# Multi-query attention on one core: rounds of scores over tiles that come free on the way, a DMA that sums two terms, and more places for weights

## The chip, the cores and the metric

The kernel runs on one core of one Trainium2 chip. The metric is device time in microseconds (us) of one launch, the median of three runs. The profile is of one more execution of the same program, with a span from the first to the last instruction of the program and, around it, a little time of the device.

## The reference

Attention with 16 query heads that share one key and one value head:

```python
batch, seq_len, embed_dim = (8, 1024, 1024)
num_heads = 16                      # head_dim = 64
# q [8, 1024, 16, 64], k and v [8, 1024, 64], float32
q = q.transpose(0, 2, 1, 3)
scores = np.matmul(q, k[:, None].transpose(0, 1, 3, 2)) / np.sqrt(head_dim)
weights = np.exp(scores - np.max(scores, axis=-1, keepdims=True))
weights = weights / np.sum(weights, axis=-1, keepdims=True)
attn_out = np.matmul(weights, v[:, None])
return attn_out.transpose(0, 2, 1, 3).astype(np.float32)
```

## The kernel before

The work is cut into 1024 *units*. A unit u is one pair of heads (64 pairs over the 8 batches), one chunk of 512 queries (2 per pair) and one tile of 128 keys (8 per chunk): it yields a score tile of 128 keys x (2 heads x 512 queries) in PSUM. Eight units in a row with the same pair and chunk make one *head* h of the plan. There are three score tiles (sc0 to sc2, two banks each); the last two banks take the results.

**Scores** (`scores`, L263): two matmuls on TensorE (PE), one per head, each on 64 rows of the array. **Weights**: the exponential of a score tile is taken in one of two ways.

- A units: ScalarE (ACT) does the whole of it in one activation (`scalar_exp`, L276) to a `wt` tile in fp16, one of `N_WT` = 22 places.
- V units: VectorE (DVE) builds it from the bits of fp16. `ve_bits` (L283) reads the scores from PSUM and writes an integer whose bits, read as fp16, are a power of two times 1 + f. `ve_mantissa` (L294) takes out the mantissa m, `ve_power` (L304) the power of two, `ve_square` (L315) makes m squared, and the product of the first with m squared is split by columns: the first part on GpSimd (POOL; `ve_cube`, L319) while VectorE is in a pass that GpSimd can run beside, the rest on VectorE (`ve_rest`, L327). Three fp16 terms lie in one `w3` tile (8 places): bits, power, cube. The exponential is their sum with fixed factors.

**Values** (`value`, L396): for each of 8 groups (4 blocks of 128 queries x 2 heads) of a head, PE multiplies every term of the head's eight units by V, 65 columns with a column that sums the weights, and adds them up in PSUM. An A unit gives one term, a V unit three. The fixed factors of the terms are in copies of V: `vps` holds V times 1, C0 and C3, made by `prep_v` (L251) for each batch. Seven groups share a result bank. `inverse` (L345) takes the reciprocals of the sums, `finish` (L354) multiplies, both on VectorE, and a store (L380) goes out on SyncE's queue (SP). `last_values` (L420) does the last head.

Loads of q (L166, with a cast to fp16) and of v (L149) go through GpSimd's queue, the transposes of q (L176) and k through SP's. GpSimd's queue thus holds cubes and loads, in order.

**What sets the order.** `plan()` walks through the work with assumed durations (`T_PAIR`, `T_IN`, `T_OUT`, `T_MM`, `T_ACT`, `VE_COST` and so on), gives every instruction a due time, and sorts by it; each engine then runs its instructions in that order and waits on semaphores where data are not there. PE alternates between *rounds* of one or more score pairs and runs of values. A round begins where at least two score tiles are free at PE's time, or where one is free and ACT would otherwise run dry:

```python
n_free = sum(f <= t_pe for f in free)
go = n_free > 1
if n_free == 1:
    other = sorted(late_free(i) for i in range(3))[1]
    go = max(other, t_pe) + T_IN + T_SCORE > t_act + WAIT and t_pe + NEAR >= t_act - T_IN - T_SCORE
```

In a round of two the second unit can go to VectorE (`VSLOT` = 1), if VectorE's backlog and the quota (`RATE`) allow. Values of a term come up when its due time plus `SAFE` = 300 ns is past.

Of the kernel before, what the change touches and what calls it, by code (L numbers as in the profile page):

```python
# [10 lines left out]
FP32 = mybir.dt.float32  # L11
FP16 = mybir.dt.float16
I32 = mybir.dt.int32
I16 = mybir.dt.int16
ALU = mybir.AluOpType
# [3 lines left out]

SUM_LO = 128.0  # L20
SUM_HI = 60000.0
C0 = 0.9833984375
C3 = 0.163818359375
CS = 2.1471603163479376
N_WT = 22
N_W3 = 8
N_M = 2
N_M2 = 3
T_PAIR = 214.0
T_IN = 96.0  # L30
T_OUT = 106.0
T_MM = 29.6
T_SCORE = 480.0
T_ACT = 917.0
ACT_DONE = 1110.0
MM_DONE = 270.0
VE_TAIL = 115.0
# [3 lines left out]
GP_COL = 1.887  # L41
GP_TAIL = 230.0
T_LOAD = {"load_q": 640.0, "load_v": 1000.0}
SIDE = (("prep_k", 58), ("prep_v", 72))
VE_COST = {
    "bits": 1141.0,
# [8 lines left out]
    "finish": 542.0,  # L55
}
ORDER = {"bits": 0, "inverse": 1, "finish": 2}
NEXT = {"bits": 0.0, "inverse": 0.0, "finish": 0.0}
MINC = 128
REST = 768  # L60
LATE = 500.0
VSLOT = 1
DEFER = 12
HOLD = 1400.0
VE_SLACK = 2500.0
V_END = 12
RATE = 0.235
NEAR = 2000.0
WAIT = -100.0
T_BITS = 1255.0  # L70
SAFE = 300.0

# [2 lines left out]
def attention_main(ctx, tc, q, k, v, out, flag):  # L75
# [11 lines left out]
    nc = tc.nc  # L87
    B, S, H, D = q.shape
    P = 128
    NKT = S // P  # L90
    QCH = 512
# [25 lines left out]
    ident16 = consts.tile([P, P], FP16, name="ident16")  # L117
    ones = consts.tile([P, 1], FP32, name="ones")
    rec_all = consts.tile([P, NG], FP32, name="rec_all")
    vps = [consts.tile([P, 3, NKT, 72], FP16, name=f"vp{i}") for i in range(2)]  # L120
    ok_all = consts.tile([P, B + GRP], FP32, name="ok_all")
    qf = consts.tile([P, NKT, P], FP32, name="qf")

    sc = {}
    ve = {}
# [25 lines left out]
        )  # L151

    def load_q_first(p):
        q16[("first", p)] = consts.tile([P, NKT, P], FP16, name=f"q16_first{p}")
        src = q[0, :, 2 * p : 2 * p + 2, :].rearrange("(c p) h d -> p c (h d)", p=P)
        if p:
            nc.gpsimd.dma_start(out=q16[("first", p)], in_=src)
            return
        for cs in (slice(0, NKT // 2), slice(NKT // 2, NKT)):
            nc.scalar.dma_start(out=qf[:, cs, :], in_=src[:, cs, :])  # L160
# [86 lines left out]

    def prep_v(b):
        vp = kv[b]["vp"]
        for i, ci in ((1, C0), (2, C3)):  # L250
            x = nc.vector.tensor_scalar(  # L251
                out=vp[:, i, :, 0:D], in0=vp[:, 0, :, 0:D], scalar1=ci, scalar2=None, op0=ALU.mult
            )
        return x
# [23 lines left out]
    def ve_bits(u, i):  # L278
        p, c, j = where(u)
        w3 = w3p.tile([P, 3, 2, QCH], FP16, tag=f"w3_{i}", name=f"we{p}_{c}_{j}")  # L280
        wt[u] = [(w3[:, 1], 0), (w3[:, 0], 1), (w3[:, 2], 2)]
        ve[u] = {"w3": w3}
        nc.vector.tensor_scalar(  # L283
            out=w3[:, 1].bitcast(I16),
            in0=sc.pop(u),
            scalar1=15.0 * 1024,
            scalar2=0.0,
            op0=ALU.add,
            op1=ALU.max,
        )  # L290

    def ve_mantissa(u, i):
        ve[u]["m"] = mp.tile([P, 2, QCH], FP16, tag=f"m{i}", name=f"m{u}")
        return nc.vector.tensor_scalar(  # L294
            out=ve[u]["m"].bitcast(I16),
            in0=ve[u]["w3"][:, 1].bitcast(I16),
            scalar1=0x3FF,
            scalar2=0x3C00,
            op0=ALU.bitwise_and,
            op1=ALU.bitwise_or,  # L300
        )

    def ve_power(u):
        return nc.vector.tensor_scalar(  # L304
            out=ve[u]["w3"][:, 0].bitcast(I16),
            in0=ve[u]["w3"][:, 1].bitcast(I16),
            scalar1=0x7C00,
            scalar2=None,
            op0=ALU.bitwise_and,
        )  # L310

    def ve_square(u, i):
# [18 lines left out]
    def after_vector(x, key):  # L331
        tc.add_manual_dep(
            x.ins,
            made[key].ins.name,
            mybir.DependencyInfo(mybir.DependencyClass.Sync, mybir.DependencyReason.DATA),
            reason="GpSimd reads beside VectorE's next pass over PSUM",
        )

    def cube_of(u):
        w3 = ve[u]["w3"]  # L340
# [117 lines left out]
        return g0, min(GB, NG - GRP - g0)  # L458

    kinds = {}  # L460

    def terms_of(h):
        us = range(h * NKT, (h + 1) * NKT)
        own = [(u, 0) for u in us]
        return own + [(u, i) for i in (1, 2) for u in us if kinds[u] == "V"]

    def plan():
        ops = []

        def emit(t, what, *args):  # L470
            ops.append((t, len(ops), what, args))

        t_pe = t_ve = t_act = t_gp = 0.0
        mode = "v"
        u = 0
        free = [0.0] * 3
# [14 lines left out]
        behind = None  # L491
        t_behind = 0.0
        loads = []
        live = {}
        h = g = n = 0
        terms = None
# [11 lines left out]
        def slot():  # L508
            return min(range(3), key=lambda i: free[i])
# [7 lines left out]
        def backlog():  # L517

            t = sum(VE_COST[k] for k, _ in chain) + VE_COST["rest"] * len(left)
            return t + sum(VE_COST[k] for _, k, _, _ in evict)  # L520

        def share(s):

            nonlocal t_gp, lock, behind
            if behind is None:
                return
            v = next((v for v in left if left[v]), None)
            if v is not None:
                gs = max(t_gp, t_behind + GP_START, squared[v] + GP_START)
                n = min(int((s - gs - GP_FIX) / GP_COL) // 32 * 32, left[v])  # L530
                if n >= MINC:
                    lo = 2 * QCH - left[v]
                    emit(gs, "cube", v, lo, lo + n, behind)
                    left[v] -= n
                    lock = gs + GP_FIX + n * GP_COL
                    t_gp = lock + GP_TAIL
                    ready[v, 2] = max(ready.get((v, "g"), 0.0), t_gp)
                    ready[v, "g"] = ready.pop((v, 2))
                    for x in loads:
                        emit(t_gp, *x)  # L540
                        t_gp += T_LOAD[x[0]]
                    loads.clear()
            behind = None

        def vector_step(limit):

# [20 lines left out]
            if not urgent and (  # L567
# [22 lines left out]
                if what == "rest":  # L590
                    n = left.pop(v)
                    done = 0.0
                    if n:
                        emit(s, "rest", v, 2 * QCH - n)
                        t_ve = s + VE_FIX + n / 1.92
                        done = t_ve + VE_TAIL
                        behind, t_behind = ("rest", v), t_ve
                    ready[v, 2] = m2_used[live.pop(("m2", v))] = max(done, ready.get((v, "g"), 0.0))
                    return True
                chain.pop(0)  # L600
                t_ve = s + VE_COST[what]
# [44 lines left out]
                    chain.append(("check", b))  # L646
            return True

        def issue(t, first):
            nonlocal u, t_act, made_v  # L650
            i = slot()
            s = max(t, free[i])
            to_v = (
                first
                and NKT <= u < STEPS - V_END
                and not todo
                and max(t_ve, s) + backlog() < s + T_SCORE + VE_SLACK
                and kinds.get(u - 1) != "V"
                and made_v < (u - NKT + 1) * RATE
                and min(w3_used) < s  # L660
            )
            if not to_v and min(wt_used) == float("inf"):
                return False
            kinds[u] = "V" if to_v else "A"
            made_v += to_v
            emit(s, "score", u, i)
            done = s + T_SCORE
            free[i] = float("inf")
            if to_v:
# [26 lines left out]
        while h < H or u < STEPS:  # L696
            guard += 1
            assert guard < 400000

            while vector_step(t_pe):  # L700
                pass
            n_free = sum(f <= t_pe for f in free)
            go = n_free > 1
            if n_free == 1:
                other = sorted(late_free(i) for i in range(3))[1]
                go = max(other, t_pe) + T_IN + T_SCORE > t_act + WAIT and t_pe + NEAR >= t_act - T_IN - T_SCORE
            if u < STEPS and go:
                t = t_pe + (T_IN if mode == "v" else 0)
                k = 0
                while u < STEPS and k < n_free and issue(t, n_free > 1 and k == VSLOT):  # L710
                    t += T_PAIR
                    k += 1
                if k:
                    rounds += mode == "v"
                    mode = "s"
                    t_pe = t
                    continue
# [39 lines left out]
            idle += 20.0  # L757
        while vector_step(float("inf")):
            pass
        assert u == STEPS  # L760
        return [(what, args) for _, _, what, args in sorted(ops, key=lambda x: x[:2])]

# [18 lines left out]
    with tc.manual_schedule():  # L781
# [6 lines left out]
        for c in range(NKT):  # L788
            load_q(0, c)
        for t in vps:  # L790
            for i, ci in enumerate((1.0, C0, C3)):
                nc.gpsimd.memset(t[:, i, :, D : D + 1], ci)
        nc.vector.tensor_copy(out=ident16, in_=ident)
        nc.vector.memset(ones, 1.0)
# [13 lines left out]
        for c in range(NKT):  # L808
# [6 lines left out]
            "power": ve_power,  # L815
            "square": ve_square,
            "cube": ve_cube,
            "rest": ve_rest,
            "load_q": load_q,
            "load_v": load_v,  # L820
# [140 lines left out]
```

## Time and profile before

| | |
|---|---|
| time, median of 3 runs | 763.36 us (762.74 to 763.97) |
| profiled execution: time / span | 762.94 us / 761.1 us |
| granted TensorE clock, mean | 0.997 |
| A units / V units | 800 / 224 |
| score matmuls (L263), value matmuls (L396) | 2048, 11712 |
| GpSimd: cubes (L319), q loads (L166), v loads (L149) | 279, 64, 8 |
| first activation starts / last one ends | 7.0 us / 752.4 us |

The page gives for each engine its busy time, share of the span and instructions. Below that, a group's line has the source line, engine, operation, tile written and tiles read, shape, count, busy time in all, the mean length of one, and the engine's idle time before them with what ended it. Instructions of one engine overlap on PE, ACT and VectorE, so the length of one is more than the distance between two. A line of waits has who waited on whom, us in all, times, and the longest. A line of the timeline has its start, its length from the first start to the last end, and a count.

### The profile page before, as it was taken

What the parts mean: (1) busy time and instruction counts of PE and PEld (TensorE: products, weight loads), DVE (VectorE), ACT (ScalarE), POOL (GpSimd) and SP (SyncE); (2) the same over time, 40 slices, a digit from 0 to 9 for tenths busy, and PEclk for the clock granted to TensorE, in tenths of its full rate; (3) what the DMA queues carried; (4) which work ended last, traced back from release to release, by engine and by line L of the source; (5) the groups of instructions that cost most, each with busy time, mean ns of one, the idle gap of its engine ahead of it and who ended that gap; (6) DMA issues with size and microseconds to landing.
All of it is one profiled execution on the core that took longest, in us unless ns stands there. A gap on an engine that the chain in (4) does not pass through costs nothing.

```text
span 761.1 us, 31746 instructions
## 1 busy us (share of the span) xinstructions
PE 746.3 (98%) x13858; PEld 480.7 (63%) x13858; DVE 728.8 (96%) x1474; ACT 747.5 (98%) x803; POOL 327.2 (43%) x364
## 2 busy tenths in 40 slices
PE   6999999999999999999999999999999999999996
PEld 3566666666666666666666666666666665666665
DVE  4999999999999999999999999999999999999994
ACT  7999999999999999999999999999999999999995
POOL 4644444443444344543444344434444334444440
PEclk9999999999999999999999999999999999999999
DMA  9964437663466525665446563467535565211112
GB/s 173 167 121 99 99 64 114 113 117 94 78 118 113 105 62 112 106 113 92 79 93 112 114 113 74 90 111 125 99 75 95 100 112 96 71 44 58 30 58 73
DMA packets 168926, 73.91 MB, mean 97 GB/s; under 512 B 94032, under 2 KB 161616, under 8 KB 168784
## 3 DMA queue, kind: packets, MB, share of 16 engines
q1 hardware_dynamic: 149152, 53.76, 32.7%
q0 software_dynamic: 18576, 17.57, 18.3%
q8 instruction: 109, 1.79, 1.1%
q10 hardware_dynamic: 1056, 0.52, 0.2%
q14 instruction: 33, 0.27, 0.1%
HBM read 37.75 MB, written 33.55 MB: 94 GB/s over the span
## 4 chain that ended last, share of the span: by engine, by line
ACT 54%; PE 42%; issue 3%; DMA 1%; DVE 1%
ACT wt L276 54%; PE ot L396 24%; PE sc L263 17%; DMA knat<-in_k_dram 0%; PE otl L420 0%; DMA out_dram<-osb 0%; DVE osb L354 0%; PE kps L200 0%; PE qps L216 0%; DVE k L191 0%; DVE rec_all L345 0%; DVE k2t L212 0%; PE cnt L837 0%; DVE okm L835 0%; DVE ok_all L443 0%
## 5 line engine op out<-in xcount | busy, mean ns | idle before, releaser
L276 ACT ACTIVATE wt<-sc 128x1024 f16<-128x1024 f32 x800 | 745.0, 1046 | 1.1 <-PE sc L263 0.9
L319 POOL TENSOR_TENSOR we<-we,mm 128x448 f16<-128x448 f16 (+4 forms) x279 | 281.9, 1010 | 409.2 <-DVE mm L315 214.4
L396 PE MATMUL ot<-vp,wt 128*128 128x65 f16 x6336 | 432.2, 194 | 0.0
L396 PE MATMUL ot<-vp,we 128*128 128x65 f16 x5376 | 432.2, 194 | 0.0
L396 PEld LDWEIGHTS <-wt 128*128 128x128 f16 x6336 | 317.4, 97 | 115.0 <-issue 115.0
L396 PEld LDWEIGHTS <-we 128*128 128x128 f16 x5376 | 316.1, 97 | 104.5 <-issue 103.4
L263 PE MATMUL sc<-qt,k2t 64*128 64x512 f16 x2048 | 354.3, 385 | 4.4 <-ACT wt L276 2.9
L283 DVE TENSOR_SCALAR we<-sc 128x1024 int16<-128x1024 f32 x224 | 272.5, 1217 | 8.7 <-PE sc L263 6.7
L315 DVE TENSOR_TENSOR mm<-m 128x1024 f16<-128x1024 f16 x224 | 151.8, 678 | 0.0
L263 PEld LDWEIGHTS <-k2t 64*128 64x128 f16 x2048 | 80.1, 93 | 48.5 <-issue 7.8
L294 DVE TENSOR_SCALAR m<-we 128x1024 int16<-128x1024 int16 x224 | 92.5, 413 | 0.2
L304 DVE TENSOR_SCALAR we<-we 128x1024 int16<-128x1024 int16 x224 | 92.5, 413 | 0.0
L354 DVE TENSOR_TENSOR osb<-ot,rec_all 128x448 f32<-128x448 f32 x146 | 89.2, 611 | 0.2
L327 DVE TENSOR_TENSOR we<-we,mm 128x576 f16<-128x576 f16 (+7 forms) x222 | 87.4, 394 | 0.0
L166 POOL DMA_DIRECT2D q<-in_q_dram x64 | 38.6, 606 | 5.5 <-issue 1.5
L345 DVE RECIPROCAL rec_all<-ot 128x7 f32<-128x7 f32 x146 | 28.7, 197 | 7.4 <-PE ot L396 6.8
L149 POOL DMA_DIRECT2D vp<-in_v_dram x8 | 7.2, 899 | 0.0
L251 DVE TENSOR_SCALAR vp<-vp 128x512 f16<-128x512 f16 x16 | 3.8, 279 | 2.2 <-DMA vp<-in_v_dram 2.2
L200 PE MATMUL kps<-ident,k 128*64 128x128 f16 x16 | 1.3, 314 | 4.4 <-DVE k L191 4.3
L234 DVE TENSOR_SCALAR k16d<-knat 128x1024 f16<-128x1024 f32 x7 | 4.7, 672 | 0.0
L229 DVE COPY qt<-qps 128x512 f16<-128x512 f16 (+1 forms) x2 | 1.1, 555 | 3.0 <-PE qps L216 3.0
L200 PEld LDWEIGHTS <-k 128*64 128x64 f16 x16 | 0.8, 158 | 4.6 <-DVE k L191 4.6
(30 smaller groups left out, 23.7 us busy)
## 6 DMA issues: line engine op xcount, KB each, us to landing
out_dram<-osb SPq DMA_DIRECT2D x109, 256.0 KB, 2.6
q<-in_q_dram POOLq DMA_DIRECT2D x56, 256.0 KB, 4.4
out_dram<-osb SPq DMA_DIRECT2D x38, 128.0 KB, 2.4
knat<-in_k_dram SPq DMA_DIRECT2D x7, 256.0 KB, 3.9
q<-in_q_dram POOLq DMA_DIRECT2D x8, 192.0 KB, 8.2
vp<-in_v_dram POOLq DMA_DIRECT2D x8, 128.0 KB, 5.8
qt<-q SPq DMA_TRANSPOSE x64, 4.8
qf<-in_q_dram ACTq DMA_DIRECT2D x2, 256.0 KB, 4.0
```

The source lines that it names most:

```text
L166: nc.gpsimd.dma_start(out=q16[(b, c)], in_=q[b, c * P : (c + 1) * P, h0:, :].rearrange("p h d -> p (h d)"),)
L263: nc.tensor.matmul(sc[u][:, hh, :], k2t[r : r + 64, j * P : (j + 1) * P], qt[b][r : r + 64, p % HP, c * QCH : (c + 1) * QCH], start=True, ...
L276: nc.scalar.activation(out=w, in_=sc.pop(u), func=EXP, scale=escale, bias=math.log(CS))
L283: nc.vector.tensor_scalar(out=w3[:, 1].bitcast(I16), in0=sc.pop(u), scalar1=15.0 * 1024, scalar2=0.0, op0=ALU.add, op1=ALU.max,)
L294: return nc.vector.tensor_scalar(out=ve[u]["m"].bitcast(I16), in0=ve[u]["w3"][:, 1].bitcast(I16), scalar1=0x3FF, scalar2=0x3C00, op0=ALU.b ...
L304: return nc.vector.tensor_scalar(out=ve[u]["w3"][:, 0].bitcast(I16), in0=ve[u]["w3"][:, 1].bitcast(I16), scalar1=0x7C00, scalar2=None, op0 ...
L315: return nc.vector.tensor_tensor(out=ve[u]["m2"], in0=m, in1=m, op=ALU.mult)
L319: x = nc.gpsimd.tensor_tensor(out=wu[:, lo:hi], in0=we[:, lo:hi], in1=mm[:, lo:hi], op=ALU.mult)
L327: return nc.vector.tensor_tensor(out=wu[:, lo:], in0=we[:, lo:], in1=mm[:, lo:], op=ALU.mult)
L345: nc.vector.reciprocal(out=rec_all[:, g0 : g0 + n], in_=o[:, 0:n, D])
L354: nc.vector.tensor_tensor(out=ob[:, i0 : i0 + n, :], in0=o[:, 0:n, 0:D], in1=rec.unsqueeze(2).broadcast_to([P, n, D]), op=ALU.mult,)
L396: nc.tensor.matmul(ots[g0][:, gg - g0, 0 : D + 1], w[:, hh, qb * P : (qb + 1) * P], kv[h // (HP * NCH)]["vp"][:, ci, u % NKT, 0 : D + 1], ...
```

## The change

It has these parts, all in the attention's main function and its plan:

- **Terms of V units.** The mantissa is set between 0.5 and 1 (0x3800 for 0x3C00), the power term gets fixed low bits by a second operation (`| 0x0201`), and the factors become: bits times KAPPA, power times 1, cube times 1. V is held in two copies (1, KAPPA) and not three; `prep_v` makes one scaled copy per batch.
- **A sum by DMA.** Of every three V units one is put in `merged`: after its cube is made, a DMA of GpSimd's queue adds its power term to its cube term (`merge`), and its values then have two terms and not three. The plan counts 650 ns of GpSimd for it and takes the sum as there 5000 ns after its issue.
- **Rounds.** A tile counts as free if it will be so, by the plan, within 90 ns of PE's time for the first, and for each next one within 50 ns of the time its pair comes up in the round. The unit for VectorE is the second of a round of two or more. A single V unit may also be a round by itself if ACT has over 1200 ns in stock and VectorE is ahead.
- **Places.** 27 for ACT's weights. The first q tiles lie in places of the wt and w3 rings that are not yet used, not in tiles of their own.
- **Constants** of the plan: durations, backlog (`VE_SLACK`), quota (`RATE` 0.24), when a rest pass is due (`REST` 576), and others.

In the order that comes out there are 802 A and 222 V units, 74 of these merged, 11088 value matmuls, and 641 rounds of scores for 744. The core of the diff:

```diff
-C0 = 0.9833984375
-C3 = 0.163818359375
-CS = 2.1471603163479376
-N_WT = 22
+KAPPA = 1.5258396029178207
+CS = 3.2766468288976904
+N_WT = 27
...
-T_PAIR = 214.0
+T_PAIR = 215.5
-T_OUT = 106.0
-T_MM = 29.6
+T_OUT = 120.0
+T_MM = 30.2
-T_ACT = 917.0
+T_ACT = 905.0
+T_MERGE = 650.0
+MERGED = 5000.0
+ADD_N = 1
+ADD_M = 3
...
-REST = 768
-LATE = 500.0
-VSLOT = 1
+REST = 576
+LATE = 0.0
+EPS = -1000000000.0
+AWAY = 1200.0
+SLACK1 = -500.0
+SOON = 50.0
+FIRST = 90.0
-HOLD = 1400.0
-VE_SLACK = 2500.0
+HOLD = 1000.0
+VE_SLACK = 1800.0
-RATE = 0.235
-NEAR = 2000.0
-WAIT = -100.0
+RATE = 0.24
+NEAR = 400.0
+WAIT = 200.0
...
-        for i, ci in ((1, C0), (2, C3)):
+        for i, ci in ((1, KAPPA),):
...
-        wt[u] = [(w3[:, 1], 0), (w3[:, 0], 1), (w3[:, 2], 2)]
+        wt[u] = [(w3[:, 1], 1), (w3[:, 0], 0), (w3[:, 2], 0)]
...
-            scalar2=0x3C00,
+            scalar2=0x3800,
...
             scalar1=0x7C00,
-            scalar2=None,
+            scalar2=0x0201,
             op0=ALU.bitwise_and,
+            op1=ALU.bitwise_or,
...
+    def merge(u):
+        w3 = ve[u]["w3"]
+        nc.gpsimd.dma_start(out=w3[:, 2], in_=w3[:, 0], accum_op=ALU.add)
...
         own = [(u, 0) for u in us]
-        return own + [(u, i) for i in (1, 2) for u in us if kinds[u] == "V"]
+        own += [(u, 1) for u in us if kinds[u] == "V" and u not in merged]
+        return own + [(u, 2) for u in us if kinds[u] == "V"]
...
+        def merge():
+            nonlocal t_gp
+            done, v = merges.pop(0)
+            s = max(t_gp, done)
+            emit(s, "merge", v)
+            t_gp = s + T_MERGE
+            ready[v, 2] = s + MERGED
...
-            n_free = sum(f <= t_pe for f in free)
+            t_in = t_pe + (T_IN if mode == "v" else 0.0)
+            n_free = 0
+            for f in sorted(free):
+                if f > (t_in + n_free * T_PAIR + SOON if n_free else t_pe + FIRST):
+                    break
+                n_free += 1
             go = n_free > 1
+            slack = VE_SLACK if go else None
             if n_free == 1:
                 other = sorted(late_free(i) for i in range(3))[1]
                 go = max(other, t_pe) + T_IN + T_SCORE > t_act + WAIT and t_pe + NEAR >= t_act - T_IN - T_SCORE
+                if t_act > t_in + AWAY and wants(t_in, SLACK1):
+                    go = True
+                    slack = SLACK1
             if u < STEPS and go:
-                t = t_pe + (T_IN if mode == "v" else 0)
+                t = t_in
                 k = 0
-                while u < STEPS and k < n_free and issue(t, n_free > 1 and k == VSLOT):
-                    t += T_PAIR
+                at_v = int(n_free > 1 and t + T_PAIR + T_SCORE > t_act + EPS)
+                while u < STEPS and k < n_free and issue(t, slack if k == at_v else None):
+                    t = t_now + T_PAIR
                     k += 1
```

## The prediction

> **What bounds the kernel now.** I read the busy times of the page first, then the busy times by stretch, the waits, and last the ACT and PE timelines. Busy shares alone do not tell:
>
> ```profile
> PE 746.3 (98%) x13858; PEld 480.7 (63%) x13858; DVE 728.8 (96%) x1474; ACT 747.5 (98%) x803; POOL 327.2 (43%) x364
> ...
> L276 ACT ACTIVATE wt<-sc 128x1024 f16<-128x1024 f32 x800 | 745.0, 1046 | 1.1 <-PE sc L263 0.9
> ```
>
> PE and ACT both look full. The stretches (PE, PEld, DVE, ACT, POOL, clock, DMA share, GB/s) say that it is so all the way:
>
> ```profile
> 60.00:160.00 100.00, 99.91 (x1871) 64.37 (x1869) 98.72 (x203) 99.99 (x109) 42.88 (x44) 1.00 0.53 100
> 460.00:560.00 100.00, 99.84 (x1871) 64.38 (x1869) 98.27 (x200) 100.00 (x109) 44.13 (x51) 1.00 0.52 95
> ```
>
> But ACT's activations overlap: one lasts 1046 ns and there is one per 745.4 us / 800 = 931 ns, so a late start hides inside the one before. ACT's timeline shows two paces:
>
> ```profile
> 7.00 7.44 ACT L276 ACTIVATE wt<-sc 128x1024 f16<-128x1024 f32 x8 [0.70 <-PE sc L263]
> ...
> 399.65 6.69 ACT L276 ACTIVATE wt<-sc 128x1024 f16<-128x1024 f32 x7
> ```
>
> At the start, with scores in stock, eight take 7.44 us: (7.44 - 1.1)/7 = 0.905 us each. In the middle seven take 6.69: (6.69 - 1.05)/6 = 0.940. Start to start no two are closer than 903 ns. The 217 activations whose scores ended within 800 ns of the start of the one before follow it at 907 ns on average; for the other 582 of 799 they ended later. So ACT is being fed late, by 24 ns apiece, and the feeder is PE. PE waits for nobody:
>
> ```profile
> PE sc L263 <- ACT wt L276: 2.9, 8, 0.5
> ...
> PE sc L263 <- DVE we L283: 0.8, 3, 0.3
> ```
>
> 3.7 us in all. Joining each score with the last reader of its tile, the tile has been free for 434 ns (median) when PE comes to it. **PE's order is the bound; tiles, ACT and VectorE are not.** What PE spends is in its timeline:
>
> ```profile
> 319.70 0.23 PE L396 MATMUL ot<-vp,wt 128*128 128x65 f16 x2
> 319.86 0.39 PE L263 MATMUL sc<-qt,k2t 64*128 64x512 f16 x2
> 320.18 0.20 PE L396 MATMUL ot<-vp,wt 128*128 128x65 f16 x1
> 320.22 0.32 PE L396 MATMUL ot<-vp,we 128*128 128x65 f16 x5
> 320.37 0.26 PE L396 MATMUL ot<-vp,wt 128*128 128x65 f16 x3
> ```
>
> Five values take 320.37 - 320.22 = 0.15 us, 30 ns each (31.2 over all 10968 steps). A round of one score pair: about 125 ns from the last value's start, 3 ns between the two matmuls, 316 to the next value, 443 in all. A further pair in the same round adds 226. So a round's turn-round costs 443 - 226 - 31 = 186 ns, once, however many pairs it holds.
>
> **The change, part by part.** Counts come from the two kernels' instruction orders.
>
> PE, values. 74 of the 222 V units have power and cube summed by a DMA, so one term fewer each: 74 x 8 = 592 matmuls; two V units fewer (222 for 224, each with two terms beyond its own) take 2 x 2 x 8 = 32 more. 11712 becomes 11088; 624 x 31.2 ns = 19.5 us off.
>
> PE, rounds. Before: 475 rounds of one pair, 264 of two, 5 longer: 744. After: 293 of one, 336 of two, 12 longer: 641. 103 x 186 ns = 19.2 us off. PE's own work is then 746.3 - 19.5 - 19.2 = 707.6 us, all of it on the path that sets the end until ACT takes over. A round now starts up to 90 ns before its first tile is due and up to 50 before the next: at most 641 x 90 ns of waiting, but PE waits there because ACT or VectorE is behind, which is spare time of PE and not of the path.
>
> ACT: 802 activations for 800. At 907 ns, 727.4 us; at today's 931.5, 747.1. PE at 708 no longer sets the pace, so **what is late next is ACT itself**. I take 912 ns: one activation in five still late by today's 24 ns, since about a fifth of the score pairs go to VectorE and shift the tiles' turn. 802 x 0.912 = 731.4 us.
>
> VectorE: two V units less, 2 x (1217 + 413 + 413 + 678) = 5.4 us; the rest passes (L327) have 99360 columns for 107488, at (684 - 305)/(1024 - 288) = 0.515 ns a column 4.2 us, and three passes fewer 0.5; eight prep_v passes fewer (one copy of V scaled, not two) 8 x 279 = 2.2. 728.8 - 12.3 = 716.5, of which about 5 lie before the first and after the last activation: 711 of 731, 97%. Least intervals between starts, summed, give some 706. It has room, but little.
>
> GpSimd: 247 cubes of 127968 columns for 279 of 121888. By the 448 (1029) and 736 (1578) rows: 1.906 ns a column, 175 fixed, so +11.6 - 5.6 = 6 us. 74 merges have no row; the nearest is the q load L166, 592 ns mostly, up to 742 beside a whole L304 pass: 74 x 0.6 = 44 us. Sum 377, half the span. Behind a waiting merge stand cubes and q loads, and PE's cube terms wait for those; the merge stands in the order after its rest pass is due, and 50% idle covers a late one. At 742 each it costs 11 us more there, nothing on the path.
>
> The merge's landing is the price that no row shows. It is 256 KB in 128 rows through GpSimd's queue, and PE's first value of that term waits for it with every later value and score queued behind. Bounds:
>
> ```profile
> q<-in_q_dram POOLq DMA_DIRECT2D x56, 256.0 KB, 4.4
> ...
> vp<-in_v_dram POOLq DMA_DIRECT2D x8, 128.0 KB, 5.8
> ...
> k2t<-k16d SPq DMA_TRANSPOSE x7, 2.7
> ```
>
> 2.7 us below (SBUF to SBUF), 6.7 above (the slowest V load after 50 us). The q load is nearest: same queue, same 2048-byte packets (172 ns, 8 on each engine), and it too reads 4096 bytes for each 2048 written, as an addition of two fp16 rows does. I take 4.4 us (5th to 95th of a hundred: 3.7 to 5.6). By the plan's due times the first use comes 5.3 to 11.0 us after issue, median 6.7. With landing x for all, the stalls of PE add up to 0 at 5.0, 1.5 us at 5.5, 10 at 5.9, 18 at 6.2, 34 at 6.7; ACT's stock bridges about 0.2 us of each. So nothing at 4.4. In the first 40 us, where the DMA engines are full, one q load took 8.1 us: a merge there may cost 2.8, which goes in the range.
>
> The Trainium skill, Collectives: The Full Stack, section The bandwidth ceiling, says an addition in a DMA emits two read descriptors per chunk on one ring and so takes twice as long as a copy. By it, as an estimate, a merge would have 16 packet times on an engine and not 8, 1.4 us more.
>
> Two copies of V, q's first tiles in places of the wt and w3 rings (read before 10 us, overwritten after 20), 27 places for 22, the second operation in the power pass (L294 has two and takes the same 413 ns as L304 with one): nothing. Longer keeping of weights only makes PE's choice of values wider.
>
> **Sum**, against the profiled execution (span 761.1, 762.94 with 1.84 around it; 0.4 under the median 763.36): first activation at 7.0, 731.4, 0.1 for the last one's length, then 761.1 - 752.4 = 8.7 of last values and stores: 747.2; with 1.84, 749.0.
>
> **Rivals.** (a) ACT is fed perfectly, 905 ns: 743.4, and 741.8 at 903. For it: eight in a row at the start did. Against: three tiles, of which VectorE holds one much of the time. Part of the forecast's spread, as is 920 ns (755.5), the next cluster of intervals in the trace.
> (b) Merges land 1.4 us later than q loads, at 5.8: stalls of 8 us, 757. For: a packet with two reads may take two packet times. Against: SBUF answers both, not HBM. That is the page's rule worked out; no run here has shown a merge.
> (c) Slower: merges land late enough to take the whole gain. 764.5 needs 15.5 us of stalls, which is a landing of 6.1 us; at 6.7 it is 749 + 34 - 5 = 778. Place: PE at the first cube value of a merged unit, then ACT. For: the slowest V load did 6.7, two reads and a write in one packet are unseen. Against: 51 q loads stayed under 5.9, and the DMA engines are half idle, 74 x 8 x 172 ns = 102 us adding 14% to 53%.
> (d) The gain does not come: with three tiles, one at VectorE, a tile's loop (written, waited for, read, freed) sets ACT's pace, and it stays at 931: 7.0 + 747.1 + 8.8 + 1.84 = 764.7, same or just slower. Against: tiles wait 434 ns for PE today, not the other way round.
> (e) The rounds do not shrink: excluded, the order has them.
>
> **How the numbers follow.** Forecast with (a): 0.74; (b) 0.10; (c) 0.11; (d) 0.05. Forecast 749. Range 742 (903 ns) to 761 (920 ns and (b)'s stalls, or 912 and a few late merges): it leaves out (c), most of (d). A difference of 0.2%, 1.5 us, is about what the runs can tell (762.74 to 763.97). Faster: forecast and (b), 0.84; same: half of (d), 0.03; slower: (c) and the rest of (d), 0.13.
>
> **What would show it.** Right: ACT's interval at 905 to 918 in the stretches (109 or 110 per 100 us instead of 107.4 starts), PE waiting on ACT's tiles for 10 to 25 us where it waits 3.7 now, no PE wait on a we DMA over 0.3 us. Wrong: merges landing after 5.8 us with PE weight loads waiting on DMA (b, c); PE waits on tiles large and ACT still at 930 (d); VectorE's bits passes starting late with VectorE at 99% would mean that VectorE, not ACT, has become the bound.

## The result and the profile after

The changed kernel takes 783.59 us (median of 4 runs, 779.38 to 785.07); the kernel before, on the same chip, 763.66 us (762.74 to 764.01). The ratio is 1.0254 [1.0209, 1.0299]: slower, where 749.0 and faster was forecast. The profiled execution took 782.14 us, with a span of 780.4 and a mean granted clock of 0.976 (0.997 before).

The page of the changed kernel, busy times and the groups of ACT and of the merge (line, engine, operation, tiles, count | busy us, mean ns | idle before, with what ended it):

```profile
PE 730.8 (94%) x13234; PEld 474.2 (61%) x13234; DVE 734.0 (94%) x1455; ACT 743.9 (95%) x805; POOL 402.5 (52%) x404
...
L289 ACT ACTIVATE wt<-sc 128x1024 f16<-128x1024 f32 x802 | 741.4, 1147 | 18.4 <-PE sc L276 17.5
...
L355 POOL DMA_DIRECT2D we<-we x74 | 67.6, 913 | 74.2 <-issue 20.5
```

PE was 98% busy and is 94%; no engine is full any more. ACT, which had been idle for 1.1 us before its activations, is idle for 18.4. The stretches (PE, PEld, DVE, ACT, POOL, clock, DMA share, GB/s) show that the loss is not spread evenly:

```profile
60.00:160.00 100.00, 93.96 (x1715) 60.85 (x1715) 98.87 (x194) 97.45 (x106) 51.94 (x51) 0.98 0.71 125
...
460.00:560.00 100.00, 93.12 (x1670) 60.68 (x1671) 91.72 (x185) 93.31 (x103) 52.93 (x52) 0.97 0.67 121
```

A count in this view takes in activations that only reach into the stretch. By their starts there are 105 and 102 in 100 us, where 109 or 110 were forecast; and the clock, 1.00 before, is 0.98 and 0.97. The stretches between (160 to 360) hold 109 starts each at 1.00. So there are places where it goes wrong. The waits (waiter <- whom it waited for: us in all, times, longest):

```profile
ACT wt L289 <- PE sc L276: 17.5, 28, 5.3
...
PE sc L276 <- ACT wt L289: 11.9, 28, 0.5
PE sc L276 <- DVE we L296: 11.8, 23, 1.4
...
PE ot L414 <- DMA we<-we: 10.1, 6, 5.0
```

PE waits for ACT's tiles as forecast (10 to 25 us). One wait is new: 10.1 us for the merges' landing, six times and up to 5.0 at a time. Another has grown: 11.8 us for tiles that VectorE still holds, where it was 0.8.

**Where 33.1 us went** (782.14 against 749.0). First activation's start to the last one's end is 759.1 us for a forecast 731.5: 27.6. After it come 75 values, where the forecast's tail, taken from before, held 4 (2.2 us more), and a longer drain of GpSimd at the program's end (3.3). The first of these was taken apart by experiments.

### The profile page after: what moved, and what is told of

Same layout as the page of the kernel before. It is cut to its first block, busy times and chain, and to the rows that moved or that the text cites. A ratio compares the mean times of both kernels' runs of the same rounds, so it can differ in the third digit from the quotient of the medians.

```text
span 780.4 us, 30889 instructions
## 1 busy us (share of the span) xinstructions
PE 730.8 (94%) x13234; PEld 474.2 (61%) x13234; DVE 734.0 (94%) x1455; ACT 743.9 (95%) x805; POOL 402.5 (52%) x404
## 4 chain that ended last, share of the span: by engine, by line
PE 45%; DVE 38%; DMA 7%; issue 6%; ACT 3%; POOL 0%; DVEq 0%; POOLq 0%; SPq 0%
PE ot L414 26%; PE sc L276 19%; DVE we L296 14%; DVE mm L329 7%; DMA we<-we 5%; DVE m L307 5%; DVE we L341 4%; DVE we L317 4%; DVE osb L372 3%; ACT wt L289 3%; DVE rec_all L363 1%; DMA out_dram<-osb 1%; DMA qf<-in_q_dram 0%; PE otl L438 0%; DVE k16d L247 0%
## 5 line engine op out<-in xcount | busy, mean ns | idle before, releaser
L289 ACT ACTIVATE wt<-sc 128x1024 f16<-128x1024 f32 x802 | 741.4, 1147 | 18.4 <-PE sc L276 17.5
L333 POOL TENSOR_TENSOR we<-we,mm 128x448 f16<-128x448 f16 (+10 forms) x247 | 297.4, 1206 | 279.3 <-DVE mm L329 84.0
L414 PE MATMUL ot<-vp,wt 128*128 128x65 f16 x6352 | 416.3, 195 | 0.0
L414 PE MATMUL ot<-vp,we 128*128 128x65 f16 x4736 | 401.6, 195 | 10.3 <-DMA we<-we 10.1
L276 PE MATMUL sc<-qt,k2t 64*128 64x512 f16 x2048 | 353.9, 389 | 25.5 <-ACT wt L289 11.9
L414 PEld LDWEIGHTS <-we 128*128 128x128 f16 x4736 | 294.5, 98 | 92.8 <-issue 89.2
L296 DVE TENSOR_SCALAR we<-sc 128x1024 int16<-128x1024 f32 x222 | 269.0, 1212 | 12.8 <-PE sc L276 11.5
L276 PEld LDWEIGHTS <-k2t 64*128 64x128 f16 x2048 | 93.0, 93 | 93.2 <-issue 50.7
L355 POOL DMA_DIRECT2D we<-we x74 | 67.6, 913 | 74.2 <-issue 20.5
L307 DVE TENSOR_SCALAR m<-we 128x1024 int16<-128x1024 int16 x222 | 100.1, 451 | 0.2
L317 DVE TENSOR_SCALAR we<-we 128x1024 int16<-128x1024 int16 x222 | 98.2, 442 | 0.0
L341 DVE TENSOR_TENSOR we<-we,mm 128x576 f16<-128x576 f16 (+16 forms) x219 | 87.2, 398 | 0.0
```

The source lines that it names most:

```text
L276: nc.tensor.matmul(sc[u][:, hh, :], k2t[r : r + 64, j * P : (j + 1) * P], qt[b][r : r + 64, p % HP, c * QCH : (c + 1) * QCH], start=True, ...
L289: nc.scalar.activation(out=w, in_=sc.pop(u), func=EXP, scale=escale, bias=math.log(CS))
L296: nc.vector.tensor_scalar(out=w3[:, 1].bitcast(I16), in0=sc.pop(u), scalar1=15.0 * 1024, scalar2=0.0, op0=ALU.add, op1=ALU.max,)
L307: return nc.vector.tensor_scalar(out=ve[u]["m"].bitcast(I16), in0=ve[u]["w3"][:, 1].bitcast(I16), scalar1=0x3FF, scalar2=0x3800, op0=ALU.b ...
L317: return nc.vector.tensor_scalar(out=ve[u]["w3"][:, 0].bitcast(I16), in0=ve[u]["w3"][:, 1].bitcast(I16), scalar1=0x7C00, scalar2=0x0201, o ...
L333: x = nc.gpsimd.tensor_tensor(out=wu[:, lo:hi], in0=we[:, lo:hi], in1=mm[:, lo:hi], op=ALU.mult)
```

## The experiments

Three causes were tested. **G**, GpSimd's queue: a merge holds GpSimd for longer than planned, and the cube behind it then runs beside VectorE passes that it blocks. **L**, the landing: PE stands at the first value of a merged unit. **C**, the clock: what G and L make PE wait lowers its granted clock, which costs again. Beside them stand that the rounds (**R**), places or constants of the plan are to blame, and that the order itself costs (**W**), because PE runs out of values while the plan counts a sum as under way. "After" below is the changed kernel; each diff is against it.

### The same order without the DMAs, and the plan without merges

The first of these leaves the power term out of the merged units' sums.

```diff
 x4_same_order_no_dma
     def merge(u):
         w3 = ve[u]["w3"]
-        nc.gpsimd.dma_start(out=w3[:, 2], in_=w3[:, 0], accum_op=ALU.add)
+        return
 e2_no_merges
-ADD_N = 1
+ADD_N = 0
```

> The changed kernel's own order, instruction for instruction, with the 74 additions by DMA left out (so the power term is missing from the merged units' sums). PE, ACT, VectorE and the cubes stand as planned, with the plan's 5000 ns of waiting still in the order. If the loss is the DMAs themselves, by GpSimd's time (G) and late landings (L): 746-753, the forecast's own price of the rest. If the order costs, because PE is made to run out of values while a sum is counted as under way (W): 757-766, with PE waiting on tiles for 20 us or more and low-clock stretches in the middle.

> The changed kernel with no V unit merged (ADD_N = 0): three terms each with two copies of V, 11680 value matmuls, new rounds and places kept. G and L: no blocked passes (under 1 us as before), no PE wait on a we DMA, clock low only at the start and the end; PE's own work 708 + 592 x 31.2 ns = 726 us, ACT the bound: 750-758. R: the loss stays, 770-785.

The same order of instructions without the 74 DMAs took 757.87 us (757.65 to 758.7), ratio 0.9929 [0.9912, 0.9945]. **The DMAs alone cost 783.59 - 757.87 = 25.7 us.** The time lies above the 746 to 753 expected if the DMAs were the whole loss, at the lower end of W's range; of W's signs, PE waits 15.9 us for tiles by the view of waits (20 or more expected), and one stretch has the low clock. The page of x4_same_order_no_dma, and one of its stretches:

```profile
PE 729.0 (96%) x13234; PEld 475.1 (63%) x13234; DVE 719.2 (95%) x1455; ACT 738.5 (98%) x805; POOL 332.4 (44%) x330
```

```profile
60.00:160.00 100.00, 97.69 (x1786) 63.53 (x1782) 98.13 (x199) 100.00 (x111) 45.13 (x44) 1.00 0.57 101
```

ACT is full, 111 where after has 106. VectorE is busy for 719.2 us where after has 734.0 for the same passes: 14.8 us of VectorE's time are made by the merges. But even this is 9 us above the forecast of 749.0, mostly by ACT's run of 738.9 us, 921 ns apiece and not 912.

With no merges in the plan either (665 rounds, 11680 values): 759.2 us (758.89 to 759.49), ratio 0.994 [0.9924, 0.9957], 1.2 us over what was expected if G and L are the loss, and far from R's 770 to 785.

### The merge in GpSimd's queue, with nobody waiting for it

Here the DMA adds into a spare tile that no one reads; the V units keep three terms. In the first it reads the power term, which has long been there; in the second the cube term, so that it must wait for the rest pass, as the real one does. The order is the same in both. The third is the second with 1400 ns planned for the merge.

```diff
 e6_merge_unused, e9_merge_of_cube_unused, x3_merge_of_cube_unused_priced
+    spare = consts.tile([P, 2, QCH], FP16, name="spare")
...
-        nc.gpsimd.dma_start(out=w3[:, 2], in_=w3[:, 0], accum_op=ALU.add)
+        nc.gpsimd.dma_start(out=spare, in_=w3[:, 0], accum_op=ALU.add)   # e6
+        nc.gpsimd.dma_start(out=spare, in_=w3[:, 2], accum_op=ALU.add)   # e9, x3
...
-T_MERGE = 650.0
+T_MERGE = 1400.0   # x3 alone
-N_WT = 27
+N_WT = 26
```

> The DMA's additions are issued as in the changed kernel, 74 of them with the same 650 ns in the plan, but into a spare tile that nothing reads; V units keep three terms (11680 value matmuls), so PE waits for no merge; 26 places for weights, not 27, to make room. G: blocked passes as in the changed kernel, 14-20 us, VectorE busy 732-737, time 765-772. L: 750-758, as without merges. R: 778-785.

> As the run whose additions go to a spare tile, but the DMA reads the cube term and not the power term: so, as in the changed kernel, a merge waits at the head of GpSimd's queue for its rest pass. T_MERGE = 650; V units keep three terms, PE waits for no merge; 26 places. G: blocked passes 14-20 us (3.1 when the merge read the power term), which is then the price of the wait in GpSimd's queue alone: time 767-774 against 763.3. L: blocked passes or not, 762-765, since ACT and PE ride over late score tiles as long as PE itself never stands.

> The run whose additions read the cube term into a spare tile (771.9 us), with T_MERGE = 1400: G alone, priced in full. Blocked passes from 23.6 us to under 4, and 760-764, as when the DMA read the power term (763.3); the rest over 757-759 is the longer drain of GpSimd at the end. If a merge in GpSimd's queue costs even where the plan knows of it: 766-771.

Measured: 763.3 us (ratio 0.9993 [0.9983, 1.0003]), 771.9 (1.0112 [1.0091, 1.0132]) and 761.52 (0.9975 [0.9964, 0.9985]). The merge's group of e6_merge_unused, and then of e9_merge_of_cube_unused with its busy times:

```profile
L356 POOL DMA_DIRECT2D spare<-we x74 | 68.9, 931 | 2.3 <-PE sc L277 1.7
```

```profile
PE 740.6 (96%) x13826; PEld 490.3 (64%) x13826; DVE 739.2 (96%) x1453; ACT 742.6 (96%) x805; POOL 399.2 (52%) x418
...
L356 POOL DMA_DIRECT2D spare<-we x74 | 67.7, 915 | 69.5 <-issue 21.4
```

The issue itself is the same, 0.92 us. (That the first is 4 us slower than e2_no_merges is for the most part a longer drain of GpSimd at the program's end, 4.7 us for 1.5. It hit none of its three ranges: G's expected 14 to 20 us of blocked passes and got 3.1, because this merge finds its term ready; the second run was made to tell the issue from the wait.) What differs is the wait at the head of the queue, 2.3 us in all against 69.5, and it costs 771.9 - 763.3 = **8.6 us though no one waits for the data**. With the merge planned at 1400 ns the 8.6 us are gone, though in a plan of its own (73 merges, 650 rounds for 663), and VectorE's busy time falls back from 739.2:

```profile
PE 741.1 (98%) x13778; PEld 490.0 (64%) x13778; DVE 719.1 (95%) x1441; ACT 741.2 (98%) x808; POOL 373.3 (49%) x387
```

This third run also moves as many bytes by DMA as the changed kernel (93 MB, 74 in e2_no_merges), and it is only 2.3 us above e2_no_merges, less than the 3.2 us by which its drain is longer. So the traffic of the merges does not cost by itself.

How a late merge reaches VectorE is in the timelines of the changed kernel, first GpSimd, then VectorE:

```profile
111.21 0.85 POOL L355 DMA_DIRECT2D we<-we  x1 [0.69 <-DVE m L307]
111.84 1.10 POOL L333 TENSOR_TENSOR we<-we,mm 128x352 f16<-128x352 f16 x1
```

```profile
110.33 0.33 DVE L341 TENSOR_TENSOR we<-we,mm 128x224 f16<-128x224 f16 x1
110.58 0.41 DVE L307 TENSOR_SCALAR m<-we 128x1024 int16<-128x1024 int16 x1
110.91 1.23 DVE L296 TENSOR_SCALAR we<-sc 128x1024 int16<-128x1024 f32 x1
112.05 1.19 DVE L317 TENSOR_SCALAR we<-we 128x1024 int16<-128x1024 int16 x1
```

The merge's own rest pass (L341) ends at 110.66, the merge starts at 111.21, 0.55 us later. The cube behind it starts at 111.84 and lasts to 112.94. It was planned to lie beside the bits pass over PSUM (110.91 to 112.14); so shifted it runs into the power pass (L317), which takes 1.19 us for its usual 0.41. The same cube and the same power pass in x4_same_order_no_dma, where no merge stands ahead:

```profile
111.11 0.85 POOL L333 TENSOR_TENSOR we<-we,mm 128x352 f16<-128x352 f16 x1 [0.71 <-PE sc L276]
```

```profile
112.16 0.42 DVE L317 TENSOR_SCALAR we<-we 128x1024 int16<-128x1024 int16 x1
```

There the cube ends at 111.96, before the power pass begins. Over the run of the changed kernel 30 such passes right behind a merge lost 16.1 us against their medians, 19.9 us with the others; 1.0 in x4_same_order_no_dma. The Trainium skill, SBUF — State Buffer, section Who interferes with whom, says that a VectorE pass using both of its port pairs and a GpSimd instruction exclude each other for a whole instruction, the one that comes first going first. The trace agrees: the power pass ends 0.3 us after the cube does, and its 0.41 us became 1.19.

### Real merges with better prices in the plan

```diff
 e1_issue_priced                e7_issue_priced_in_full
-T_MERGE = 650.0               -T_MERGE = 650.0
+T_MERGE = 1000.0              +T_MERGE = 1400.0
 e3_landing_late                e8_both_priced
-MERGED = 5000.0               -T_MERGE = 650.0
+MERGED = 6500.0               -MERGED = 5000.0
                               +T_MERGE = 1400.0
                               +MERGED = 6500.0
```

> The changed kernel with T_MERGE = 1000 for 650: the plan counts on GpSimd what a merge really takes there (913 ns mean, plus its waits). Theory G (GpSimd's time): the cubes behind a merge start late and lie beside VectorE's passes over SBUF, which then last until the cube ends; in the changed kernel 30 passes lost 16 us to cubes right behind a merge, 20 us in all such losses. With the right price that falls under 4 us, VectorE's busy time from 734 to about 719, time to 765-772. Theory L (landing): what costs is PE waiting for the few merges that land late (10 us in 6 waits) and the lower clock after each; this edit leaves the landing, so 778-785. Theory R (rounds): the new rounds are what costs; 778-785.

> The changed kernel with MERGED = 6500 for 5000: the plan lets 1.5 us more pass before PE uses a sum. L: PE's waits on merges fall from 10 us and more to under 3, low-clock stretches in the middle vanish, time 768-773. G: VectorE's blocked passes stay at 15-20 us, time 775-782. R: 780.

> The changed kernel with T_MERGE = 1400: in the run with 1000 a merge still started 0.55 us after its own term was there and took 0.92 us, so GpSimd is taken for 1.45 us from the end of the rest pass where the plan has 0.115 + 1.0. G: blocked VectorE passes at last under 4 us (13.7 with 1000, 19.9 with 650), VectorE busy 718-722. L: PE's waits on merges stay near 10 us with four or more low-clock stretches in the middle, so time 768-776. If blocked passes were the larger part: 758-766.

> The changed kernel with T_MERGE = 1400 and MERGED = 6500. If G and L together are the whole loss: blocked passes under 4 us, PE's waits on merges under 3 us, ACT's mean interval 915-920, time 752-760, at or under the run without merges. If something else of the merges costs (DMA traffic, SBUF), 765 or more.

| | us | ratio | VectorE blocked, us | PE stalled at merged terms, us (times) |
|---|---|---|---|---|
| after | 783.59 | 1.0254 [1.0209, 1.0299] | 19.9 | 11.3 (10) |
| e1, issue 1000 ns | 777.95 | 1.0172 [1.014, 1.0205] | 13.7 | 11.3 (10) |
| e3, landing 6500 ns | 776.66 | 1.017 [1.0133, 1.0207] | 17.9 | 5.5 (5) |
| e7, issue 1400 ns | 770.24 | 1.009 [1.0064, 1.0116] | 2.6 | 3.8 (5) |
| e8, both | 774.82 | 1.015 [1.0122, 1.0178] | 4.1 | 4.1 |

(Blocked: what VectorE's SBUF passes took above their medians. Stalled: from the end of the step before to the start of the first value of a merged term; it counts more places than the view of waits.) The full issue price takes 13.4 us off, the landing price 6.9. Neither is the price of one cause alone, since each new plan moves the other loss too: e7 also brings the stalls from 11.3 to 3.8 us. At 1000 ns (e1) most of the blocking stays, and the time missed G's 765 to 772. e3 came out in G's range (775 to 782), not in L's: it halves the stalls, but four stretches ahead of the tail have the low clock. e7 is within its 768 to 776. The two prices don't add up: e8 was expected at 752 to 760 if G and L are the whole loss, and at 765 or more if something else costs, and came out at 774.8. With little left of G and L, PE still waits 19.2 us there for ACT's tiles, in 46 places, and five stretches ahead of the tail have the low clock. The plan with both prices orders the work in a way that leaves PE idle. Part of it may be in the plan itself: the time in which PE has nothing due, which `plan()` adds up as `idle`, is 29 us for e7 and 37 for e8. That this is the cause is not shown.

The landing itself is as forecast in the middle and not at its end. The page's DMA part of the changed kernel (KB each, median us from issue to landing):

```profile
we<-we POOLq DMA_DIRECT2D x74, 256.0 KB, 4.1
q<-in_q_dram POOLq DMA_DIRECT2D x56, 256.0 KB, 4.6
```

Of the 74, the 30 issued with no load close before and no transpose of q in flight took 3.7 us (median) and at most 5.3; the 18 issued within 3.5 us behind a q or v load and beside a transpose took 5.4, up to 11.3. The latest, in GpSimd's timeline, then in the chain of waits from 500 to 530 us, then at PE:

```profile
499.74 0.59 POOL L179 DMA_DIRECT2D q<-in_q_dram  x1
500.33 1.04 POOL L161 DMA_DIRECT2D vp<-in_v_dram  x1
501.36 0.92 POOL L355 DMA_DIRECT2D we<-we  x1
```

```profile
501.36 11.26 DMA we<-we
```

```profile
507.35 0.39 PE L276 MATMUL sc<-qt,k2t 64*128 64x512 f16 x2 [0.52 <-ACT wt L289]
512.75 0.21 PE L414 MATMUL ot<-vp,we 128*128 128x65 f16 x1 [5.01 <-DMA we<-we]
...
513.72 0.61 PE L276 MATMUL sc<-qt,k2t 64*128 64x512 f16 x2
```

A merge right behind two loads lands 11.26 us after its issue, PE stands for 5.01 us with every later score behind it (the prediction's own test was 0.3), and the next score pair comes 6.4 us after the one before. Its two matmuls take 0.61 us for 0.39: this is C. The same stretch in the changed kernel, then in x4_same_order_no_dma (columns as above, the clock third from the end):

```profile
511.50:518.30 6.80, 5.55 (x70) 3.85 (x72) 2.84 (x7) 2.96 (x3) 2.49 (x3) 0.50 0.62 136
```

```profile
511.50:518.30 6.80, 6.80 (x122) 4.43 (x121) 6.80 (x14) 6.80 (x9) 5.43 (x5) 1.00 1.05 137
```

3 activations start there, 8 without the DMAs, and the clock is half. The changed kernel has six such stretches ahead of its tail, 3.41 or 6.83 us long, 30.7 us together; 19 activations started in them where 34 fit at 904 ns, which is 13.5 us, part of it the stalls themselves. The starts of the stretches lie whole multiples of 3.41 us apart. Ahead of each of the six, PE had waited for 0.55 to 1.0 of such a window (what its steps took beyond 31 ns a value, 125 into a round, 226 a pair, 319 out of it); after the first 15 us, the fullest window with no drop behind it was 0.49. Four of the six follow a stall at a merged term; ahead of those at 23 and 365 us PE waits for no merge. x4 has one ahead of its tail, at 27 us; e9, whose losses are many and short, none. The Trainium skill, TensorE: Matmul & The Clock Gate, section What's actually happening, says that the clock halves after an idle window of about 3.4 us. The trace agrees with the length and the halving; but the windows ahead of five of the six were not idle: 0.55 to 0.60 of them was enough.

### Rounds, places and constants

```diff
 e5_old_rounds_no_merges, e10_22_places
-ADD_N = 1
+ADD_N = 0
...
-                if f > (t_in + n_free * T_PAIR + SOON if n_free else t_pe + FIRST):
+                if f > t_pe:
...
-N_WT = 27
+N_WT = 22          # e10 alone
 x5_merge_free
-T_MERGE = 650.0
-MERGED = 5000.0
+T_MERGE = 0.0
+MERGED = 0.0
...
-        nc.gpsimd.dma_start(out=w3[:, 2], in_=w3[:, 0], accum_op=ALU.add)
+        return
```

> The changed kernel without merges and with the count of free tiles as before (a tile counts only if it is free at PE's time): 705 rounds for 665 without merges and 744 before. Rounds theory: 40 rounds more x 186 ns = 7.4 us of PE's work, and PE sets the pace again: 763-767 against 759.2. If the rounds give nothing and the gain comes from places and constants: 757-761.

> The run with old rounds and no merges (757.2 us), with 22 places for ACT's weights as before in place of 27. If the places bring the gain over the kernel before: 761-764, with PE choosing values from a shorter stock. If the plan's other constants do (backlog, quota, rest): 756-759, and a shorter tail of values after the last activation (50 with 27 places, 4 before).

> The same with T_MERGE = 0 and MERGED = 0: the plan counts the sum as there at once, the DMA is left out (the power term is missing from the merged units' sums). What fewer value matmuls would give if a merge cost nothing. If PE's 18 us of values are worth what the forecast said: 744-752. If ACT cannot be fed at 912 ns whatever PE has to do: 755-760, as without merges.

e5 took 757.24 us (0.9921 [0.9905, 0.9938]) with 705 rounds, e10 757.2 (0.9914 [0.9898, 0.9931]) with 698, x5 754.68 (0.9886 [0.987, 0.9903]).

Rounds: e2 differs from e5 by the new count of free tiles alone. It has 40 rounds fewer, 7.4 us at 186 ns each, and is 2 us slower: PE waits for tiles within rounds for 15.6 us in e2, 7.0 in e5, because the second score of a round often comes before its tile is free. The turn-round that is saved is spent as a wait. Places: e10 is as fast as e5 with 22 of them. With 27 places more values are left after the last activation (50 in e5, 92 in e2, none in e10; the kernel before, with 22, has 4). So the 6.4 us that e5 gains over the kernel before come from the rest of the change, the terms and the plan's constants (744 rounds became 705); no run separates these two. e10 and e5 are faster than both kernels.

x5 is what a sum that costs nothing would give at best: its order has no delay for merges and no DMA, and the power term is left out of the merged units' sums. It came out between its two ranges (744 to 752, 755 to 760), and 3.2 us under x4, whose order has the delay. That is 4.5 us under e2, which has the same rule for rounds, and 2.6 under e5: with ACT at 920 ns apiece, PE's 592 matmuls less (18.5 us) are worth little.

### Fewer merges, and merges away from loads

```diff
 e11_old_rounds_with_merges, e12_few_merges_old_rounds, e15_merges_away_from_loads
-T_MERGE = 650.0
+T_MERGE = 1400.0
...
-                if f > (t_in + n_free * T_PAIR + SOON if n_free else t_pe + FIRST):   # e11, e12
+                if f > t_pe:
...
-ADD_M = 3          # e12
+ADD_M = 6
...
-            s = max(t_gp, done)                  # e15; t_load is GpSimd's time after a load
+            s = max(t_gp, done, t_load + 3500.0)
```

> All 74 merges priced in full (T_MERGE = 1400) with the old count of free tiles: 666 rounds, 11072 value matmuls. If what still costs beside merges is PE standing idle in the new rounds and losing its clock (770.2 with new rounds): 760-765, at most one low-clock stretch in the middle. If PE's waits on merges cost by themselves: 766-772, with low-clock stretches right behind waits on a we DMA.

> One V unit of six merged (38 merges), priced in full, old rounds: 11392 value matmuls, 320 fewer than without merges, 10 us of PE's own work, which set the pace in the run without merges (757.2). If a merge that is priced in full costs nothing but its late landings: 752-756, with half of the final drain's extra 3.3 us. If each merge costs more than the 0.25 us of values that it saves: 758-764.

> The changed kernel with T_MERGE = 1400 and merges put off until 3.5 us after the last q or v load of GpSimd's queue: in the changed kernel the 18 merges issued within 3.5 us behind a load and beside a transpose of q took 5.4 us (median) and up to 11.3 to land, the 30 with neither 3.7 and at most 5.3. L by its queue: landings over 6.2 us vanish, PE waits on merges under 2 us (5.7 with the price alone), fewer low-clock stretches than 3; time under 770.2, but no less than 762, since the plan holds terms longer. If landings stay as they are, the queue in front is not the reason.

e11: 776.17 us (1.0163 [1.0143, 1.0184]), 2.0 us blocked, 7.7 us stalled: slower than both its ranges (760 to 765, 766 to 772), and 5.9 us slower than e7 with the new rounds. e12, with 38 merges: 781.69 (1.0242 [1.0209, 1.0275]), 3.3 blocked, 12.8 stalled in 9 places; expected below 764 by either theory, so a miss. Its PE comes for a sum 5.6 us (median) after the issue, where after it is 6.5, and a landing of 7.8 (95th of a hundred) is then late more often, with six low stretches of the clock and 18.7 us of ACT waiting for scores. Half as many merges do not cost half. e15: 776.03 (1.0161 [1.0141, 1.0182]). The stalls at merged terms go (1.2 us, 3). 8 merges are still issued close behind a load and beside a transpose (18 in the changed kernel), and 3 still land after 6.2 us (6 in the changed kernel, all six within 1.8 us behind a q load). So a load close ahead goes with a late landing here too, though late ones do not vanish as expected. The time missed its 762 to 770: PE waits 23.6 us for ACT's tiles and five stretches have the low clock, as in e8. The plans of e11 and e15 leave PE with nothing due for 40 and 42 us.

So the DMAs' 25.7 us are shown as a whole, and G by itself (8.6 us with nobody waiting for the data). L and C are seen in the traces, the stalls behind late landings and the low stretches behind the stalls, but no run gives the price of either alone. Of the 25.7 us, 13.4 go when the issue has its price. Of the 12.4 us from x4_same_order_no_dma to e7, 3.3 are the drain and 3.8 the stalls that are left; that the rest, about 5, is lost next to the low clock is not shown. Why the plans of e8, e11, e12 and e15 leave PE idle in more places stays open.

## Why the prediction was wrong, point by point

- **"50% idle covers a late one", "nothing on the path"** (GpSimd): this step failed, and the one part of the loss that is shown by itself hangs on it (8.6 us in e9, up to 13.4 in e7). The issue was sized at 592 ns to 742; it took 913, beyond both ends, and started 0.55 us after its term was there. More than the size, the cover was the wrong one: what stands behind a merge is a cube that has to meet one certain pass of VectorE. An engine's idle half does not cover an order in which each instruction has its neighbour on another engine. VectorE came to 734.0 us for a forecast 716.5 (719.2 without the DMAs).
- **"So nothing at 4.4"** (the landing): the median was right (4.1), its use was not. The stalls come from the slow end: 18 of 74 at 5.4 and up to 11.3 us, beside loads that the plan puts right ahead. The stalls worked out for one landing of all, 10 us at 5.9, were met by a median of 4.1 with a long tail (11.3 us). The rival (c) had this mechanism and place, at 778 for a landing of 6.7 for all; it had a chance of 0.11. The one q load of 8.1 us was set aside as a thing of the first 40 us.
- The same stalls were priced one for one on ACT's path. No term stood for the clock, which takes up to 13.5 us, part of it the stalls themselves. The profile of before had one sign: its clock of 0.997 holds one low stretch of 3.41 us, at 12 us.
- **802 x 0.912**: ACT's pace came to 921 ns without any DMA, 7.4 us over the run, the upper end that rival (a)'s paragraph named (920). The scores come late because of the tiles: 301 of them ended 800 to 850 ns after the start of the activation before. PE waits 33 us there between the pairs of a round, 7 in the kernel before: the forecast called such waiting spare time of PE. That is rival (d)'s tile loop at part of its price; 904 was held where scores lay in stock.
- **The tail, "8.7"**, was taken as unchanged. 75 values are left after the last activation for 4 (2.2 us), and the drain is 3.3 us longer. More places let values pile up (none left in e10 with 22, 50 in e5 with 27), but not alone: x5, with 27, has none.
- What held: PE's own work, 709 us in x4 (741.8 from the first score to the last value, less the 33 of waiting in rounds) for 707.6, and with it the 31.2 ns a value; GpSimd's work without merges (332.4 us, 333 in the sum); PE's wait for ACT's tiles (11.9 us); that a packet with an addition takes hardly longer than one of a load (178 ns for 173, medians), so that rival (b)'s doubling did not bear. The Trainium skill, Collectives: The Full Stack, section The bandwidth ceiling, gives the doubling for the reduce step of a ring; the traces here do not agree for this DMA.
- The upper bound, 761, is below the first pair of terms named for it: 755.5 at 920 ns and (b)'s 8 us of stalls make 763.5. The measured time lies far outside either.

## What to carry to other kernels

Before an operation is put into a queue that is half idle, look at what the instructions behind it must meet: where an order interleaves two engines pass by pass, a delay in one can cost the other as much again (0.73 us late for the cube shown, 0.78 us more for the pass). Price a transfer that a saturated in-order engine waits for at the slow end of its landings, with loads next to it in its queue, and not at the median; and look at the granted clock, because here four of the stalls were followed by 3.4 or 6.8 us at half speed. Ask first what the removed work is worth with a free substitute: here 18.5 us of matmuls were worth 2.6 to 4.5.

## What the runs showed of the hardware that was not expected

GpSimd's drain at the end of the program is longer in the kernels with merges. First the changed kernel, then the kernel before (shortest/median/longest ns):

```profile
L1013 POOLq DRAIN  x3: 44/107/4724, 774.8 to 780.1; - x3
```

```profile
L956 POOLq DRAIN  x3: 40/107/1457, 758.7 to 760.9; - x3
```

It takes 1457 ns with 73 DMAs of GpSimd (in six kernels), 4357 with 111 (e12), 4642 with 146 and 4724 with 147, so not in proportion. The last DMA is over 120 us before the drain in the first group and 14 to 21 us before it in the others, so that these runs cannot tell the count from the time since the last one; among those with 147 that time makes no difference.

And PE's clock was halved behind windows that were not idle. Across the runs, after the first 15 us, drops came behind windows of 3.41 us in which PE waited for 0.43 to 1.0 of the time, and the fullest window without a drop behind it had 0.61. So these runs give no sharp border: none below 0.43, all above 0.61.
